# Projections of a two-layer hybrid trunk: products and transpositions one step later, norm weights in the rotation tables, roots applied by ScalarE

## The chip, the core and the metric

The kernel is one program on one core of a Trainium2 chip. The metric is the device time of one execution in microseconds (us). The engines are TensorE (PE; its weight loads are listed apart as PEld), VectorE (DVE), ScalarE (ACT), GpSimd (POOL) and SyncE (SP), which here mainly issues transfers (DMA). Each engine works through its own instructions in a fixed order.

## The reference

Two layers run over 1152 tokens (128 context, 1024 latent) of width 1024. Each modulates and normalises its input, projects it to four groups of heads, and joins them by one output projection. What the change touches is the modulation `silu(c) @ w_ada[l] + b_ada[l]`, the projection, and the head norm and rotation of grouped-query attention (GQA), beside the two norms of multi-head latent attention (MLA):

```python
shift, scale, gate = jnp.split(mod, 3, axis=-1)
h = rms_norm(x, p['norm_pre']) * (1 + scale) + shift
u = h @ p['w_in']
...
qa = rms_norm(gq.reshape(B, N, GQA_HEADS, HEAD_DIM), p['gqa_q_norm'])
ka = rms_norm(gk.reshape(B, N, GQA_KV_HEADS, HEAD_DIM), p['gqa_k_norm'])
...
qa_use = apply_axial_rope(qa, cos_h, sin_h)
...
cq = rms_norm(mcq, p['mla_q_norm'])
ckv = rms_norm(mckv, p['mla_kv_norm'])
```

The normalised context keys of GQA, unrotated, are an output as well (`o_gqa_k`).

## The kernel before

Tokens are worked in 9 tiles of 128. float32 products are made of three passes over high and low parts: `hh`, `hl` are the two parts of the modulated input, `whi`, `wlo` those of the weights (DVE casts `whi`, L235; POOL subtracts for `wlo`, L239; each from a loaded `wst`). A layer projects group after group: GLA values, SSD gates, MLA gates, the convolution's input (`proj_T`), GQA, MLA, then the query and key groups (QK); after these come attention and the two streams, and the output projection. `proj_tok` does 24 matmuls per token tile into one of four PSUM buffers taken in turn (two of `psA`, two of `psB`), hands the buffer to `consume`, and then draws one or two steps of `steps_`. So tile 4 of a projection needs the buffer that the consumer of tile 0 has read to its end.

`steps_` is the modulation for later: while layer 0 projects, `ada_steps` makes layer 0's gate and all of layer 1's modulation, in eight parts. A part takes eight loads `ast` of 256 KB (L163), each multiplied by the condition and summed to `acc` on DVE (L173), with ACT (L167, L170) and POOL (L171) beside it; then PE sums over the partitions into `psC`, which has one buffer (L180 for the gate, L186 else). Attention's `po` uses `psC` too.

The consumer of GQA, per tile: ACT copies the values to `vg` (L557) and squares the rest to `sq` (L559); DVE reduces to `ss` (L561); POOL makes the reciprocal roots (`rstd`, L106 and L107); DVE multiplies them onto the PSUM tile to `z` (L564), which is the last reading of that buffer; POOL multiplies `z` by the norm weights `g6` (L566); with a loaded tile `ropes` DVE (L574) and POOL (L577, twice) make the two parts of the rotation, DVE adds them to `r` (L581); PE transposes `r` to `gT` (L584), and ACT copies that to `qT` and `kT`.

The code gives no order between engines' instructions: a scheduler that models the engines' times fixes each engine's order when the program is built, so that a small edit can move rows far from it. Pools with `bufs=n` give out n buffers in turn; a new tile waits for the last reader of the old.

## Time and profile before

| | before |
|---|---|
| median of 3 runs | 1848.38 us (1847.5, 1848.38, 1854.49) |
| profiled execution, its own time | 1848.65 us |
| its span | 1846.8 us |
| PE busy | 1720.3 us (93%) |
| DVE busy | 1191.8 us (65%) |
| ACT busy | 867.2 us (47%) |
| POOL busy | 740.6 us (40%) |

Busy is the time in which an engine had an instruction under way; all four run side by side, so the shares are of the same span. Times in the trace count from the start of the span. The granted clock of PE stands as a share of its full 2.4 GHz, so 0.50 is its lower level, 1.2 GHz. In a row of the trace `out<-in` names the tiles by the program's names, and a releaser behind an arrow is what ended an engine's idle time.

### The profile page before, as it was taken

What the parts mean: (1) busy time and instruction counts of PE and PEld (TensorE: products, weight loads), DVE (VectorE), ACT (ScalarE), POOL (GpSimd) and SP (SyncE); (2) the same over time, 40 slices, a digit from 0 to 9 for tenths busy, and PEclk for the clock granted to TensorE, in tenths of its full rate; (3) what the DMA queues carried; (4) which work ended last, traced back from release to release, by engine and by line L of the source; (5) the groups of instructions that cost most, each with busy time, mean ns of one, the idle gap of its engine ahead of it and who ended that gap; (6) DMA issues with size and microseconds to landing.
All of it is one profiled execution on the core that took longest, in us unless ns stands there. A gap on an engine that the chain in (4) does not pass through costs nothing.

```text
span 1846.8 us, 25193 instructions
## 1 busy us (share of the span) xinstructions
PE 1720.3 (93%) x8200; PEld 1321.0 (72%) x8200; DVE 1191.8 (65%) x2302; ACT 867.2 (47%) x1914; POOL 740.6 (40%) x911
## 2 busy tenths in 40 slices
PE   6999989999999998999999999999999999999998
PEld 2787977887665666656777999889666666665676
DVE  7627888566877887782455357543686878677233
ACT  5634422433654665583443152232465477557322
POOL 4633238852444444330334323771344454333011
PEclk9999998999999999999999999999998999899999
DMA  8434453333332331142434332131332232114243
GB/s 290 134 97 139 140 158 90 106 111 99 109 99 73 87 97 49 38 149 60 143 118 129 99 101 86 56 101 43 111 117 84 68 98 86 46 38 149 80 143 114
DMA packets 179684, 190.99 MB, mean 103 GB/s; under 512 B 29406, under 2 KB 140720, under 8 KB 179552
## 3 DMA queue, kind: packets, MB, share of 16 engines
q1 hardware_dynamic: 174208, 179.11, 31.9%
q10 hardware_dynamic: 5344, 10.26, 1.8%
q8 instruction: 65, 1.06, 0.2%
q14 instruction: 67, 0.55, 0.1%
HBM read 141.00 MB, written 48.30 MB: 103 GB/s over the span
## 4 chain that ended last, share of the span: by engine, by line
PE 36%; DVE 11%; DMA 7%; POOL 4%; ACT 3%; issue 3%; SPq 0%; POOLq 0%; DVEq 0%; ACTq 0%
PE psP L245 11%; PE op L245 8%; PE st L1057 3%; PE po L1073 3%; DVE mx L711 2%; DMA R<-d_rec 2%; PE mx L710 1%; DVE Pl L1065 1%; DMA d_rec<-rc 1%; PE po L1069 1%; DMA wst<-in_w_in_dram 1%; PE po L1067 1%; PE po L1068 1%; POOL ss L107 1%; POOL sq L577 1%
## 5 line engine op out<-in xcount | busy, mean ns | idle before, releaser
L711 DVE TENSOR_REDUCE mx<-mx 128x1 f32<-128x512 f32 (+2 forms) x400 | 224.5, 582 | 93.6 <-PE mx L710 92.0
L245 PE MATMUL psP<-whi,hh 128*128 128x512 f32 (+2 forms) x576 | 204.9, 366 | 5.6 <-DVE whi L235 4.3
L245 PE MATMUL psP<-wlo,hh 128*128 128x512 f32 (+2 forms) x576 | 204.8, 363 | 3.4 <-POOL wlo L239 2.8
L245 PE MATMUL psP<-whi,hl 128*128 128x512 f32 (+2 forms) x576 | 188.4, 360 | 0.0
L239 POOL TENSOR_TENSOR wlo<-wst,whi 128x512 fp32r<-128x512 f32 (+3 forms) x106 | 128.9, 1224 | 141.5 <-DVE whi L235 82.4
L245 PE MATMUL psP<-hh,whi 128*128 128x384 f32 x480 | 163.0, 339 | 4.7 <-DVE whi L235 3.7
L1057 PE MATMUL st<-QA,KA 128*128 128x512 f32 (+1 forms) x336 | 165.2, 492 | 0.6 <-DVE Pl L1065 0.4
L245 PE MATMUL psP<-hl,whi 128*128 128x384 f32 x480 | 160.2, 335 | 0.0
L245 PE MATMUL psP<-hh,wlo 128*128 128x384 f32 x480 | 155.0, 337 | 0.1
L1065 DVE TENSOR_TENSOR Pl<-st,Ph 128x512 fp32r<-128x512 f32 x160 | 109.7, 686 | 67.2 <-ACT st L1063 66.0
L1062 ACT ACTIVATE Ph<-st 128x512 fp32r<-128x512 f32 x160 | 95.5, 597 | 111.2 <-PE st L1057 104.4
L1072 ACT ACTIVATE P<-st 128x512 f32<-128x512 f32 (+1 forms) x176 | 99.7, 567 | 74.4 <-PE st L1057 65.3
L1057 PE MATMUL st<-QB,KB 66*128 66x512 f32 (+3 forms) x336 | 133.2, 401 | 0.0
L245 PEld LDWEIGHTS psP<-wlo,hh 128*128 128x128 f32 x576 | 111.5, 195 | 21.3 <-POOL wlo L239 6.8
L245 PEld LDWEIGHTS psP<-whi,hh 128*128 128x128 f32 x576 | 111.6, 195 | 20.0 <-DVE whi L235 6.1
L245 PEld LDWEIGHTS psP<-whi,hl 128*128 128x128 f32 x576 | 109.5, 194 | 12.0
L1057 PEld LDWEIGHTS st<-QA,KA 128*128 128x128 f32 x336 | 65.8, 196 | 50.2 <-issue 39.8
L245 PEld LDWEIGHTS psP<-hh,whi 128*128 128x128 f32 x480 | 90.1, 188 | 11.9 <-DVE whi L235 5.6
L1057 PE MATMUL st<-QB,KA 96*128 96x512 f32 (+1 forms) x168 | 93.6, 557 | 2.2 <-ACT P L1072 1.8
L1063 ACT ACTIVATE st<-st 128x512 f32<-128x512 f32 x160 | 94.9, 593 | 0.0
L235 DVE CAST whi<-wst 128x512 fp32r<-128x512 f32 (+3 forms) x114 | 74.0, 662 | 31.8 <-DMA wst<-in_w_in_dram 19.2
L1073 PE MATMUL po<-P,vm 128*65 128x512 f32 (+1 forms) x176 | 88.9, 587 | 4.6 <-ACT P L1072 2.3
(361 smaller groups left out, 4315.6 us busy)
## 6 DMA issues: line engine op xcount, KB each, us to landing
ast<-in_w_ada_dram SPq DMA_DIRECT2D x96, 256.0 KB
wst<-in_w_in_dram SPq DMA_DIRECT2D x64, 256.0 KB
wost<-in_w_out_dram SPq DMA_DIRECT2D x16, 512.0 KB
d_xs<-d_xb SPq DMA_DIRECT2D x32, 192.0 KB
ot<-d_oT SPq DMA_DIRECT2D x18, 320.0 KB
d_tok<-vv SPq DMA_DIRECT2D x18, 256.0 KB
d_gt<-gg SPq DMA_DIRECT2D x24, 192.0 KB
g_qk<-d_qk SPq DMA_DIRECT2D x36, 128.0 KB
```

Source lines behind the costliest of these rows:

```text
L107: pool.tensor_tensor(out=rs, in0=rs, in1=mhalf[:, 0:c], op=ALU.pow)
L235: dve.tensor_copy(hi[:, 0:n], st[:, 0:n])
L239: eng.tensor_tensor(out=lo[:, 0:n], in0=st[:, 0:n], in1=hi[:, 0:n], op=ALU.subtract)
L245: pe.matmul(p, lhsT=lt, rhs=rh, start=(first and i == 0), stop=(last and i == n - 1))
L577: pool.tensor_tensor(out=ws_[:, :, x, :].rearrange("p (h y) f -> p h y f", y=2), in0=zs[:, :, 1 - x, :].rearrange("p (h y) f -> p h y f", ...
L711: dve.tensor_reduce(out=mx[:, t, i:i + 1], in_=p[:, 0:n], axis=AX.X, op=ALU.max)
L1057: anchors["pe"] = pe.matmul(sp_[:, 0:nq], lhsT=kx[:, ks], rhs=qx[:, qs], start=(i == 0), stop=(i == len(spasses) - 1))
L1062: act.activation(out=Ph[:, 0:nq], in_=sp_[:, 0:nq], func=AF.Exp, scale=scale)
L1063: anchors["act"] = act.activation(out=sp_[:, 0:nq], in_=sp_[:, 0:nq], func=AF.Exp, scale=scale)
L1065: anchors["dve"] = dve.tensor_tensor(out=Pl[:, 0:nq], in0=sp_[:, 0:nq], in1=Ph[:, 0:nq], op=ALU.subtract)
L1072: anchors["act"] = act.activation(out=P[:, 0:nq], in_=sp_[:, 0:nq], func=AF.Exp, scale=scale)
L1073: pe.matmul(po[0:65, 0:nq], lhsT=v[:, kt, vi, :], rhs=P[:, 0:nq], start=(j == 0), stop=last, skip_group_check=True)
```

## The change

Four edits. (1) `ast` has three buffers instead of two, and `ada_steps` yields once more between a part's last load and its product. (2) `consume` may return a function `rest`; `proj_tok` calls it after the next tile's matmuls. For GQA and MLA it holds the transpositions and the copies out of them. (3) The rotation table of all nine tiles is loaded at once, twice (`rg[0]` for queries, `rg[1]` for keys), and multiplied by the norm weights: the cosine halves in one product of 128x9x64 each (DVE for `rg[0]`, POOL for `rg[1]`), the sine halves in four products of 128x9x16 each on POOL. The product of every tile's `z` by `g6` goes, except that tile 0 makes one of 128x128 for `o_gqa_k`; per tile the rotation is two DVE and four POOL instructions where it was one and two. (4) The reciprocal roots are applied by ACT, one instruction of 128x64 for each of six heads, instead of one of 128x384 on DVE.

```diff
             o = part * D + half * 512
             acc = wpool.tile([128, 2, 512], F32, name="acc", tag="acc", bufs=1)
-                st = wpool.tile([128, 512], F32, name="ast", tag="ast", bufs=2)
+                st = wpool.tile([128, 512], F32, name="ast", tag="ast", bufs=3)
...
                 yield
+            yield
             p = psC("ada")
...
+        rest = None
...
             mm3(p[:, 0:n], pairs)
-            consume(t, p)
+
+            last, rest = rest, consume(t, p)
+            if last is not None:
+                last()
             for _ in range(2 - t % 2):
                 next(steps_[0], None)
+        if rest is not None:
+            rest()
...
+            rg = [wk.tile([128, T, 2, 64], F32, name="rg", tag=x) for x in ("c1h", "c1l")]
+            for i in range(2):
+                sp.dma_start(out=rg[i], in_=a["rope"][:, 0:128].rearrange("(t p) (y d) -> p t y d", p=128, d=64))
+            for i in range(2):
+                gi = g6[:, i * 256:i * 256 + 64]
+                gx = gi.rearrange("p (y x f) -> p y x f", x=2, f=16)
+                (pool if i else dve).tensor_tensor(out=rg[i][:, :, 0, :], in0=rg[i][:, :, 0, :], in1=gi.unsqueeze(1).to_broadcast([128, T, 64]),
+                                                   op=ALU.mult)
+                for x in range(2):
+                    for y in range(2):
+                        o = 32 * y + 16 * x
+                        z = rg[i][:, :, 1, o:o + 16]
+                        pool.tensor_tensor(out=z, in0=z, in1=gx[:, y, 1 - x, :].unsqueeze(1).to_broadcast([128, T, 16]), op=ALU.mult)
             def cons_gqa(t, p):
                 kt = 0 if t == 0 else t + 2
-                ropes = wk.tile([128, 192], F32, name="ropes", tag="ropes", bufs=2)
-                sp.dma_start(out=ropes, in_=a["rope"][t * 128:(t + 1) * 128, :])
                 act.copy(vg[:, kt, :, 0:64], p[:, 384:512].rearrange("p (h d) -> p h d", d=64))
                 sq = wk.tile([128, 384], F32, name="sq", tag="sq", bufs=2)
                 act.activation(out=sq, in_=p[:, 0:384], func=AF.Square)
@@ -561,29 +581,35 @@
                 dve.tensor_reduce(out=ss, in_=sq.rearrange("p (h d) -> p h d", d=64), axis=AX.X, op=ALU.add)
                 rstd(ss, ss, 64, 6)
                 z = wk.tile([128, 384], F32, name="z", tag="z", bufs=2)
-                dve.tensor_tensor(out=z.rearrange("p (h d) -> p h d", d=64), in0=p[:, 0:384].rearrange("p (h d) -> p h d", d=64),
-                                  in1=ss.unsqueeze(2).to_broadcast([128, 6, 64]), op=ALU.mult)
-                pool.tensor_tensor(out=z, in0=z, in1=g6, op=ALU.mult)
+                for h in range(6):
+                    c = slice(h * 64, h * 64 + 64)
+                    act.activation(out=z[:, c], in_=p[:, c], func=AF.Identity, scale=ss[:, h:h + 1])
+                r = wk.tile([128, 384], F32, name="r", tag="r", bufs=2)
                 if t == 0:
-                    act.dma_start(out=a["o_gqa_k"][l], in_=z[:, 256:384])
+                    pool.tensor_tensor(out=r[:, 256:384], in0=z[:, 256:384], in1=g6[:, 256:384], op=ALU.mult)
+                    act.dma_start(out=a["o_gqa_k"][l], in_=r[:, 256:384])
                     act.dma_start(out=a["o_gqa_v"][l].rearrange("t (h d) -> t h d", d=64), in_=vg[:, 0, :, 0:64])
-                r = wk.tile([128, 384], F32, name="r", tag="r", bufs=2)
-                zs = z.rearrange("p (h x f) -> p h x f", x=2, f=16)
-                ws_ = sq.rearrange("p (h x f) -> p h x f", x=2, f=16)
-                rs_ = ropes[:, 64:128].rearrange("p (y x f) -> p y x f", x=2, f=16)
-                dve.tensor_tensor(out=r.rearrange("p (h d) -> p h d", d=64), in0=z.rearrange("p (h d) -> p h d", d=64),
-                                  in1=ropes[:, 0:64].unsqueeze(1).to_broadcast([128, 6, 64]), op=ALU.mult)
-                for x in range(2):
-                    pool.tensor_tensor(
-                        out=ws_[:, :, x, :].rearrange("p (h y) f -> p h y f", y=2),
-                        in0=zs[:, :, 1 - x, :].rearrange("p (h y) f -> p h y f", y=2),
-                        in1=rs_[:, :, x, :].unsqueeze(1).to_broadcast([128, 6, 2, 16]), op=ALU.mult)
+                    r = wk.tile([128, 384], F32, name="r", tag="r", bufs=2)
+                for i, (o, n) in enumerate(((0, 4), (256, 2))):
+                    c = slice(o, o + n * 64)
+                    dve.tensor_tensor(out=r[:, c].rearrange("p (h d) -> p h d", d=64), in0=z[:, c].rearrange("p (h d) -> p h d", d=64),
+                                      in1=rg[i][:, t, 0, :].unsqueeze(1).to_broadcast([128, n, 64]), op=ALU.mult)
+                    zs = z[:, c].rearrange("p (h y x f) -> p h y x f", x=2, y=2, f=16)
+                    ws_ = sq[:, c].rearrange("p (h y x f) -> p h y x f", x=2, y=2, f=16)
+                    rs_ = rg[i][:, t, 1, :].rearrange("p (y x f) -> p y x f", x=2, f=16)
+                    for x in range(2):
+                        pool.tensor_tensor(out=ws_[:, :, :, x, :], in0=zs[:, :, :, 1 - x, :],
+                                           in1=rs_[:, :, x, :].unsqueeze(1).to_broadcast([128, n, 2, 16]), op=ALU.mult)
                 dve.tensor_tensor(out=r, in0=r, in1=sq, op=ALU.add)
-                tp = psD("gT")
-                for i in range(3):
-                    pe.transpose(tp[:, i * 128:(i + 1) * 128], r[:, i * 128:(i + 1) * 128], ident)
-                act.copy(qT[:, :, t * 128:(t + 1) * 128], tp[:, 0:256].rearrange("p (a b) -> p a b", b=128))
-                act.copy(kT[:, kt * 128:(kt + 1) * 128], tp[:, 256:384])
+                def rest():
+                    tp = psD("gT")
+                    for i in range(3):
+                        pe.transpose(tp[:, i * 128:(i + 1) * 128], r[:, i * 128:(i + 1) * 128], ident)
+                    act.copy(qT[:, :, t * 128:(t + 1) * 128], tp[:, 0:256].rearrange("p (a b) -> p a b", b=128))
+                    act.copy(kT[:, kt * 128:(kt + 1) * 128], tp[:, 256:384])
+                return rest
...
-                tp = psD("mT")
...
+                def rest():
+                    tp = psD("mT")
+                    pe.transpose(tp[:, 0:128], z[:, 0:128], ident)
+                    pe.transpose(tp[0:64, 128:256], z[:, 128:192], ident)
+                    pe.transpose(tp[:, 256:384], z[:, 192:320], ident)
...
+                return rest
```

Lines after the change stand 1 to 30 higher. Three places show how rows moved.

At the start of layer 0's GQA, the rows of SP before (transfers in the order of issue; `d_bc` is the convolution's output, `wst` of 128x352 are MLA's weights):

```order
L163 DMA ast<-in_w_ada_dram 128x512
L535 DMA d_bc_430<-yc 128x128
L536 DMA d_bc_430<-yc 128x1024
L163 DMA ast<-in_w_ada_dram 128x512
L233 DMA wst<-in_w_in_dram 128x352
L556 DMA ropes<-in_rope_dram 128x192 x2
L163 DMA ast<-in_w_ada_dram 128x512
L233 DMA wst<-in_w_in_dram 128x352
```

and now:

```order
L234 DMA wst<-in_w_in_dram 128x352
L542 DMA d_bc_430<-yc 128x128
L543 DMA d_bc_430<-yc 128x1024
L234 DMA wst<-in_w_in_dram 128x352
L563 DMA rg<-in_rope_dram 128x9x128 x2
L635 DMA ropes<-in_rope_dram 128x192 x2
L116 DMA bc<-in_b_col_dram 128x16
L163 DMA ast<-in_w_ada_dram 128x512 x8
```

The two tables stand after both MLA weights, and the `ast` loads that were mixed with the weights stand behind the tables. At the same place POOL had, from GQA's last weights on:

```order
L239 TENSOR_TENSOR wlo<-wst,whi 128x512 x8
L106 TENSOR_SCALAR ss_2491<-ss_2491 128x6
L107 TENSOR_TENSOR ss_2491<-ss_2491,mhalf 128x6
L106 TENSOR_SCALAR ss_2549<-ss_2549 128x6
L107 TENSOR_TENSOR ss_2549<-ss_2549,mhalf 128x6
L566 TENSOR_TENSOR z<-z,g_1037 128x384
L577 TENSOR_TENSOR sq<-z,ropes 128x12x16 x2
L566 TENSOR_TENSOR z<-z,g_1037 128x384
```

and has now:

```order
L240 TENSOR_TENSOR wlo<-wst,whi 128x512 x8
L573 TENSOR_TENSOR rg<-rg,g_1037 128x9x16 x4
L567 TENSOR_TENSOR rg<-rg,g_1037 128x9x64
L573 TENSOR_TENSOR rg<-rg,g_1037 128x9x16 x4
L106 TENSOR_SCALAR ss_2491<-ss_2491 128x6
L106 TENSOR_SCALAR ss_2550<-ss_2550 128x6
L107 TENSOR_TENSOR ss_2491<-ss_2491,mhalf 128x6
L107 TENSOR_TENSOR ss_2550<-ss_2550,mhalf 128x6
L601 TENSOR_TENSOR sq<-z,rg 128x8x16 x2
L589 TENSOR_TENSOR r<-z,g_1037 128x128
L601 TENSOR_TENSOR sq<-z,rg 128x4x16 x2
```

All nine products of the tables stand ahead of the first reciprocal root (the small step L106 and the root L107), and the tiles' products with `g` have gone.

In layer 1's GQA POOL had:

```order
L239 TENSOR_TENSOR wlo<-wst,whi 128x512 x8
L106 TENSOR_SCALAR ss_11451<-ss_11451 128x6
L107 TENSOR_TENSOR ss_11451<-ss_11451,mhalf 128x6
L106 TENSOR_SCALAR ss_11501<-ss_11501 128x6
L107 TENSOR_TENSOR ss_11501<-ss_11501,mhalf 128x6
L566 TENSOR_TENSOR z<-z,g_10181 128x384 x2
L577 TENSOR_TENSOR sq<-z,ropes 128x12x16 x4
```

and has now:

```order
L240 TENSOR_TENSOR wlo<-wst,whi 128x512 x8
L106 TENSOR_SCALAR ss_11524<-ss_11524 128x6
L107 TENSOR_TENSOR ss_11524<-ss_11524,mhalf 128x6
L573 TENSOR_TENSOR rg<-rg,g_10242 128x9x16 x4
L106 TENSOR_SCALAR ss_11575<-ss_11575 128x6
L601 TENSOR_TENSOR sq<-z,rg 128x8x16
L589 TENSOR_TENSOR r<-z,g_10242 128x128
L601 TENSOR_TENSOR sq<-z,rg 128x8x16
L567 TENSOR_TENSOR rg<-rg,g_10242 128x9x64
L573 TENSOR_TENSOR rg<-rg,g_10242 128x9x16 x4
L107 TENSOR_TENSOR ss_11575<-ss_11575,mhalf 128x6
L601 TENSOR_TENSOR sq<-z,rg 128x4x16 x2
```

Four table products stand between the first tile's root and the second tile's small step; the other five stand ahead of the second tile's root.

At the start of layer 0's attention, PE had from the last modulation product on (`st` are score matmuls, `mx` the same for the maxima, `po` the products with the values):

```order
L245 MATMUL psP<-hh,wlo 128x384
L180 MATMUL ada<-acc,pick 2x512
L1057 MATMUL st<-QA_3697,KA_3695 128x128
L1057 MATMUL st<-QB_3698,KB_3696 128x128
L710 MATMUL mx<-KA_3695,QA_3697 128x512 x2
L710 MATMUL mx<-KA_3695,QA_3697 128x256
L1057 MATMUL st<-QA_3697,KA_3695 128x512
L1057 MATMUL st<-QB_3698,KB_3696 128x512
L1057 MATMUL st<-QA_3697,KA_3695 128x512
L1057 MATMUL st<-QB_3698,KB_3696 128x512
L1073 MATMUL po<-P,vg 65x128
```

and has now, further down its list:

```order
L1087 MATMUL st<-QB_3724,KB_3722 128x512
L757 MATMUL mT<-identr,m 2x128
L740 MATMUL mx<-KA_3721,QA_4372 128x512
L181 MATMUL ada<-acc,pick 2x512
L1087 MATMUL st<-QA_3723,KA_3721 128x512
L1087 MATMUL st<-QB_3724,KB_3722 128x512
L740 MATMUL mx<-KA_3721,QA_4372 128x512
L1103 MATMUL po<-P,vg 65x128
L1103 MATMUL po<-P,vg 65x512
L1097 MATMUL po<-Ph,vh 65x512
```

The last modulation product stood ahead of the first 512-wide `st`; now the scores of several blocks are ahead of it (those rows are left out here), and the first `po` follows it.

## Rows read from the trace of the kernel before

**Rows 1.** Windows: busy us of PE, PEld, DVE, ACT, POOL; PE clock, DMA, GB/s

```profile
140.00:285.00 145.00, 135.56 (x709) 120.45 (x708) 115.37 (x159) 54.22 (x93) 50.03 (x53) 0.95 0.48 143
285.00:335.00 50.00, 43.20 (x209) 36.42 (x208) 39.23 (x54) 12.44 (x34) 45.67 (x46) 0.93 0.38 107
1155.00:1205.00 50.00, 48.06 (x236) 40.34 (x235) 29.42 (x42) 11.42 (x35) 41.48 (x50) 1.00 0.22 63
```

**Rows 2.** Waits of PE in 130-145, 260-285, 285-335, 1180-1250: us, times, longest

```profile
PE ada L180 <- DVE acc L173: 3.2, 1, 3.2
...
PE ada L186 <- DVE acc L173: 3.9, 1, 3.9
...
PE gT L584 <- DVE r L581: 4.4, 2, 2.6
PE psP L245 <- DVE whi L235: 1.7, 3, 0.7
...
PE gT L584 <- DVE r L581: 1.1, 1, 1.1
PE psP L245 <- DVE z L564: 0.9, 2, 0.7
```

**Rows 3.** Windows, columns as in rows 1, around three of PE's waits

```profile
136.60:143.40 6.80, 6.23 (x20) 4.52 (x20) 1.60 (x5) 1.99 (x5) 1.27 (x1) 0.50 0.35 110
277.44:283.40 5.96, 5.96 (x15) 4.70 (x16) 5.09 (x6) 1.33 (x2) 5.80 (x7) 0.50 0.34 94
314.10:317.50 3.40, 3.40 (x13) 3.04 (x12) 2.10 (x4) 0.84 (x2) 3.40 (x5) 0.50 0.20 53
```

**Rows 4.** Waits of DVE in 110-138: us, times, longest

```profile
DVE acc L173 <- DMA ast<-in_w_ada_dram: 8.6, 6, 3.9
```

**Rows 5.** Timeline, 262-278: start, us, engine, line, op [idle before <-releaser]

```profile
262.92 1.68 POOL L239 TENSOR_TENSOR wlo<-wst,whi 128x512 fp32r<-128x512 f32 x1 [1.02 <-issue]
...
265.17 0.33 SPq L163 DMA_DIRECT2D ast<-in_w_ada_dram  x1
...
268.54 2.84 DVE L173 SCALAR_TENSOR_TENSOR acc<-ast,cc,acc 128x512 f32<-128x512 f32 x4 [1.88 <-DMA ast<-in_w_ada_dram]
...
275.00 0.21 POOL L106 TENSOR_SCALAR ss<-ss 128x6 f32<-128x6 f32 x1 [10.40 <-DVE ss L561]
275.29 1.34 POOL L107 TENSOR_TENSOR ss<-ss,mhalf 128x6 f32<-128x6 f32 x1
...
277.44 0.77 PE L245 MATMUL psP<-whi,hh 128*128 128x512 f32 x1
```

**Rows 6.** Timeline of PE at the start of layer 0's attention

```profile
440.90 1.07 PE L1073 MATMUL po<-P,vg 128*65 128x512 f32 x2 [1.48 <-ACT Ou L1084]
```

**Rows 7.** ACT by form: busy us, mean ns | idle before; and two copies in the timeline

```profile
L218 ACT ACTIVATE h<-hT,sc,ac 128x128 f32<-128x128 f32 x36 | 15.4, 455 | 18.9 <-DVE h L221 18.6
L167 ACT ACTIVATE acc<-ast,cc 128x512 f32<-128x512 f32 x4 | 2.7, 714 | 7.8 <-PE ada L186 7.8
...
271.32 0.44 ACT L557 COPY vg<-psP 128x128 f32<-128x128 f32 x2
```

**Rows 8.** The page's part 3: queue, packets, MB, share of 16 engines

```profile
q1 hardware_dynamic: 174208, 179.11, 31.9%
```

**Rows 9.** POOL by form, 1150-1250, columns as in rows 7

```profile
L577 POOL TENSOR_TENSOR sq<-z,ropes 128x192 f32<-128x192 f32 x18 | 14.2, 810 | 0.2
L566 POOL TENSOR_TENSOR z<-z,g 128x384 f32<-128x384 f32 x9 | 9.0, 1014 | 0.7 <-DVE z L564 0.7
L629 POOL TENSOR_TENSOR r<-z,ropes 128x16 f32<-128x16 f32 x18 | 3.6, 220 | 0.0
```

**Rows 10.** Timeline of SP, POOL and PE in layer 1's GQA

```profile
1158.43 8.57 SPq L556 DMA_DIRECT2D ropes<-in_rope_dram  x4
...
1158.18 0.21 POOL L106 TENSOR_SCALAR ss<-ss 128x6 f32<-128x6 f32 x1 [4.50 <-DVE ss L561]
...
1169.28 0.49 PE L584 MATMUL gT<-ident,r 128*128 128x128 f32 x3
```

More of the change, by code (lines that the diff above doesn't have):

```diff
@@ L630, in cons_mla @@
                 pool.tensor_tensor(out=kr, in0=kr, in1=r[:, 0:32], op=ALU.add)
-                tp = psD("mT")
-                pe.transpose(tp[:, 0:128], z[:, 0:128], ident)
-                pe.transpose(tp[0:64, 128:256], z[:, 128:192], ident)
-                pe.transpose(tp[:, 256:384], z[:, 192:320], ident)
-                s = slice(t * 128, (t + 1) * 128)
-                act.copy(c1h[:, s], tp[:, 0:128])
-                dve.tensor_tensor(out=c1l[:, s], in0=tp[:, 0:128], in1=c1h[:, s], op=ALU.subtract)
-                act.copy(c2s[0:64, s], tp[0:64, 128:256])
-                dve.tensor_tensor(out=c2s[64:128, s], in0=tp[0:64, 128:256], in1=c2s[0:64, s], op=ALU.subtract)
-                s = slice(kt * 128, (kt + 1) * 128)
-                act.copy(ckh[:, s], tp[:, 256:384])
-                dve.tensor_tensor(out=ckl[:, s], in0=tp[:, 256:384], in1=ckh[:, s], op=ALU.subtract)
+                def rest():
[3 more added lines that the diff above has]
+                    pe.transpose(tp[:, 256:384], z[:, 192:320], ident)
+                    s = slice(t * 128, (t + 1) * 128)
+                    act.copy(c1h[:, s], tp[:, 0:128])
+                    dve.tensor_tensor(out=c1l[:, s], in0=tp[:, 0:128], in1=c1h[:, s], op=ALU.subtract)
+                    act.copy(c2s[0:64, s], tp[0:64, 128:256])
+                    dve.tensor_tensor(out=c2s[64:128, s], in0=tp[0:64, 128:256], in1=c2s[0:64, s], op=ALU.subtract)
+                    s = slice(kt * 128, (kt + 1) * 128)
+                    act.copy(ckh[:, s], tp[:, 256:384])
+                    dve.tensor_tensor(out=ckl[:, s], in0=tp[:, 256:384], in1=ckh[:, s], op=ALU.subtract)
+                return rest
             proj_tok(l, hh, hl, wp, G_MLA, 352, cons_mla)
```

## The prediction

> **What bounds the kernel now.** I read the busy table, then the stages by windows, then the waits of TensorE (PE) stage by stage, then single engines where a wait ended. PE is busy 93% of the span, so only its gaps and its time at the lower clock can be won. The windows say where: in 140 to 285 us PE is busy 135.6 of 145, but in 285 to 335, the GQA and MLA projections of layer 0, 43.2 of 50, while POOL is busy 45.7 of 50; in layer 1 the same stage has PE at 48.1 of 50 and POOL at 41.5 [rows 1]. The waits name the links [rows 2]: a modulation product waits 3.2 us for DVE's sum at 137; another 3.9 us at 270 to 274; at the end of GQA the `gT` transpositions wait 4.4 us for the rotated `r`, and weights 1.7 us for DVE's casts; layer 1 has 1.1 and 0.9 us. After such waits PE's granted clock is 0.50, its lower level, for some microseconds [rows 3]. Half of PE's busy time in such a stretch is the most that full clock would give back: 3.1 us of 6.23 after the first wait (I take 2.5, since part of that busy time is the product's own pass at the wait's end), 3.0 of 5.96 after 277.44, 1.7 at 314 and, in a like stretch, 1.7 at 331.
>
> All the waits and clock losses that the change can touch are thus 3.2 + 2.5, 3.9 + 3.0, 6.1 + 3.4 and 2.0: 24 us, or 1.3%, is the ceiling.
>
> **The change part by part.** I sum against the profiled run's 1848.65 us (span 1846.8), which stands 0.3 above the median of 1848.38.
>
> *Third `ast` buffer.* Ahead of the product at 137 DVE waited 8.6 us, 6 times, for `ast` loads [rows 4]: with two buffers a load is issued only when a sum frees one. A load takes from its issue at 265.17 to DVE's use at 268.54, 3.4 us [rows 5]. With one more in flight the chain of eight loses about one such load, which covers the 3.2 us. The product stands at almost the same PE row before and after, so the wait should vanish with its half clock: -5.7 us (0 if POOL's sums were the limit, -6.3 with all the clock).
>
> *Products one step later.* The extra yield moves work back: eight parts of eight loads and two yields need 80 steps where layer 0's projections offer 72, so the last part is drained at the end of QK. PE's rows show the last product only after the first `st` of attention, and every `po` behind it, because `psC` has one buffer. There PE already waited, 1.5 us at 440.90 for ACT [rows 6]. I give this +1 us (0 if ACT and DVE set the pace anyway; +4 if one last load of 3.4 us lies bare).
>
> *`z` on ACT.* DVE loses one multiplication per tile, ACT gets six of 128x64. The trace has no such row. The nearest, ACT with a scale per partition: 128x128 0.455 us, 128x512 0.714 [rows 7]; slope 0.67 ns per element, so 0.41 for 64. Six would be 2.5 us end to end. Two ACT copies of 128x128 at 271.32 took 0.44 us together though one takes 0.27: they overlap by 0.10, so I take 1.9; at the copies' spacing of 0.17 six would be 1.1, the lower bound. ACT was idle over half of these stages, so only the delay counts: a PSUM buffer comes free, and the rotation starts, about 1.3 us later than by DVE's 0.56.
>
> The Trainium skill ("ScalarE: Activation LUTs", Rules for kernel authors) speaks against this edit: it gives multiplications to VectorE and budgets about 0.3 us per ACTIVATE plus 0.83 ns per element, by which six would take 2.1 us (an estimate from that page). Its price is inside the bounds from the rows; by it each of the two GQA starts below comes 0.2 us later, and the sum ends at -7.8 instead of -8.2. No run here yet shows 64 columns.
>
> *Folded tables.* Two loads of 590 KB in 512-byte pieces (1152 each) replace nine of 96 KB. Queue q1's 174208 packets of 1028 bytes on average took 31.9% of 16 engines' span, 54 ns each [rows 8]; 1152 over 16 engines are 3.9 us at that price and 1.9 if time goes with bytes. The 3.4 us of an `ast` load, less the 0.9 us of its packets at 54 ns and 1028 bytes, leave 2.5 us of delay. The first table then lands 4.4 us after its issue, the second 1.9 later (at the upper bounds 6.4 and 3.9). On POOL stand eight multiplications of 9x16 and one of 9x64: 16 elements took 0.220 us, 192 took 0.810, 384 in one piece 1.014 [rows 9]. Between these, 144 take 0.65 and, on the last slope of 2.16 ns, 576 take 1.43: 6.6 us of setup per layer (bounds 5.5 if all had that slope, 7.3 at twice the fixed part). Per tile the product with `g6` goes (1.01), but four rotations of 128 and 64 elements (0.60 and 0.38 by the same rows) cost 1.96 where two of 192 cost 1.62. POOL wins 0.67 us per tile, 6 us in nine: no more than the setup costs. What matters is when it is paid.
>
> *Layer 0, GQA start.* POOL stood idle 10.4 us before its first `rstd` at 275.00 [rows 5], so the setup is partly free. SP issues the tables after the second MLA weight, which needs the last GQA `wlo`. That began at 262.92 [rows 5]; its cast no longer stands behind sums, so I put `wlo`'s end at 262.2 and the tables' issue at 262.6. First table 267.0; four products to 269.6; 1.43 to 271.0; four more to 273.6; two `rstd` steps and a root of 1.34 to 275.3; `z` to 277.2. Tile 4 needs `z` of tile 0 for its PSUM buffer. Before it started at 277.44 [rows 5], behind the 3.9 us wait and 16 products at half clock. So the wait for the product goes and a wait for `z` of the same length takes its place: -0.2 (-2 to +4). That is the step that most people would book as a gain.
>
> *Layer 0, tail.* From here POOL, busy 91% of this stage before, has 0.67 us less per tile, the four sums of L171 stand later, and the transpositions are issued after the next tile's matmuls. POOL is through at least 6 us earlier, which is all that the waits for `r` and the weights came to, and PE's own 24 matmuls per tile set the pace. Of 6.1 + 3.4 I take -8 (-4 to -9.5).
>
> *Layer 1, GQA start.* No modulation, and before no PE gap. Now POOL's rows put the first four table products ahead of tile 1's `rstd`, and the other five ahead of its root. The tables take the place of `ropes` at 1158.43 [rows 10]: landing 1162.8, four products 1165.4, two rotations, the `o_gqa_k` product and a small step (1.9) 1167.3, 9x64 1168.7, four products 1171.3, root 1172.6, two rotations 1173.4, DVE's sum 1174.0. `gT` of tile 0 stood at 1169.28 [rows 10] and now waits to 1174.1; tile 5 waits for `z` of tile 1, 1174.5. That is +5.0 us (+2.5 to +7), +1.7 for the clock that sinks after it, and, since PE is then later than POOL's end, -2.0 for the tail's two waits [rows 2]: +4.7.
>
> Sum: -5.7 + 1.0 - 0.2 - 8.0 + 4.7 = -8.2, so **1840.4 us**. The order of attention and streams in layer 0 is rescheduled too; I have no row that prices it and keep 5 us to each side for it.
>
> **Rivals.** A difference under 0.5% (9.2 us) can't be told from no change.
>
> *The setup is hidden* (0.15). If the tables land early and the small products cost less than 0.5 us, layer 1 keeps its gapless start, layer 0's tile 4 starts some 5 us earlier, and both tails go whole: -5.7 + 1 - 5 - 9.4 - 2 = -21, 1827.5. For it: POOL's 10.4 idle us. Against it: in layer 1 POOL was idle only 4.5 us before its first `rstd` [rows 10], and the tables can't start before `d_bc` is written.
>
> *The stalls only change their name* (0.25). At the upper bounds of the table loads, layer 0's start costs +3, its tail gives -6, layer 1 +7: -5.7 + 1 + 3 - 6 + 7 = -0.7, 1848. For it: all setup stands in front of `rstd`, the head of the chain.
>
> *Slower* (0.14). The mechanism is the table landing late in both layers, as SP holds it behind weights that wait for POOL. POOL is in order, so `rstd`, `z`, the PSUM buffers and PE wait with it, microsecond for microsecond in each layer. From -8.2 it takes (8.2 + 9.2) / 2 = 8.7 us in each to be slower by 0.5%: a landing at 276 and 1171.5. The bounds above give only about 3.4; I keep the chance for that and the unpriced order of attention. At 11 us late it is 1862.
>
> **How the numbers follow.** The forecast has 0.46, with its own range 1835 to 1846. Of it two fifths (0.19) lie below 1839.2; with the hidden setup (0.15) and a little of the second rival (0.02) faster gets 0.36. Slower gets 0.14 + 0.02, no change 0.48. The range 1828 to 1854 leaves out half of the first rival (0.08) and most of the last (0.12).
>
> **What would show it.** No wait before the product at 137, the granted clock there 1.0; a PE gap of 4 to 8 us before tile 4 of GQA in layer 0, ended by ACT's `z`; no `gT` gaps after it; in layer 1 a new gap of about 5 us at `gT` or tile 5; six ACT instructions of 0.3 to 0.41 us per tile; table products of 0.65 us on POOL. It is wrong if tile 4 starts before 273 or after 282 (in these coordinates, less the shift from 137), if layer 1 shows no gap, or if attention of layer 0 moves by more than 5 us.

## The result and the profile after

The changed kernel takes 1860.07 us (median of 16 runs, 1853.36 to 1867.45) where the kernel before takes 1847.14 in as many; the ratio is 1.0072 with a 95% interval of 1.0055 to 1.0089. It is slower, outside the range I had given. Its profiled execution, with a span of 1853.8 us against 1846.8, is one of its quicker ones, 7 us above the profiled one of before where the medians differ by 13. The four stages below add up to +10.6; the rest of the kernel, mostly what follows in layer 1, is 3.6 us shorter.

Windows over the stages, first of the changed kernel: layer 0 from its first projection to GQA, from GQA to the end of QK, attention with streams and output projection, and layer 1 from GQA to the end of QK. Columns as in [rows 1].

```profile
46.20:232.90 186.70, 178.72 (x998) 159.98 (x997) 120.73 (x205) 88.44 (x171) 79.10 (x83) 0.99 0.44 133
232.90:421.90 189.00, 175.64 (x926) 154.89 (x925) 118.58 (x202) 68.16 (x223) 112.19 (x156) 0.95 0.38 110
421.90:972.90 551.00, 505.94 (x2209) 348.48 (x2208) 383.31 (x790) 310.01 (x656) 211.01 (x250) 0.96 0.30 93
1147.60:1317.90 170.30, 163.82 (x867) 147.48 (x866) 82.19 (x156) 54.73 (x202) 86.76 (x145) 0.97 0.24 71
```

The same four stages of the kernel before:

```profile
46.60:243.50 196.90, 184.46 (x997) 163.35 (x996) 124.89 (x204) 88.58 (x171) 77.76 (x83) 0.96 0.42 124
243.50:435.20 191.70, 179.88 (x928) 157.54 (x928) 130.38 (x205) 58.83 (x172) 115.99 (x140) 0.96 0.37 111
435.20:967.70 532.50, 497.63 (x2208) 344.90 (x2206) 370.01 (x783) 306.91 (x653) 201.28 (x245) 0.98 0.31 95
1141.70:1307.00 165.30, 160.80 (x867) 144.57 (x866) 87.63 (x155) 43.38 (x148) 88.06 (x126) 1.00 0.24 71
```

The projections of layer 0 give 10.2 and 2.7 us back. Layer 1's cost 5.0. But the third stage, whose code the change does not touch, takes 18.5 us more: for the same matmuls (2209 and 2208) PE is busy 8.3 us longer, at a lower clock, and idle 45.1 instead of 34.9. That alone turns a gain into a loss.

PE's waits after, in 125 to 135, 260 to 300, 300 to 345 and 1147 to 1250, answering to [rows 2]:

```profile
PE ada L181 <- DVE acc L173: 0.9, 1, 0.9
...
PE psP L246 <- ACT z L586: 8.4, 1, 8.4
...
PE mT L660 <- DVE z L641: 3.3, 1, 3.3
...
PE gT L608 <- DVE r L603: 4.0, 1, 4.0
```

The product's wait at 137 is nearly gone, and so are the `gT` waits of GQA's tail in layer 0. New are a wait for ACT's `z` in the place of that for the second product, one of MLA's transposition, and one of layer 1's first `gT`.

The timeline at layer 0's GQA start, which answers to [rows 5]; the second fence shows layer 1, which answers to [rows 10]:

```profile
251.31 1.79 SPq L563 DMA_DIRECT2D rg<-in_rope_dram  x2
...
256.62 2.34 POOL L573 TENSOR_TENSOR rg<-rg,g 128x144 f32<-128x144 f32 x4 [5.71 <-DMA rg<-in_rope_dram]
259.10 1.40 POOL L567 TENSOR_TENSOR rg<-rg,g 128x576 f32<-128x576 f32 x1
260.46 3.16 POOL L573 TENSOR_TENSOR rg<-rg,g 128x144 f32<-128x144 f32 x4
...
264.60 2.64 POOL L107 TENSOR_TENSOR ss<-ss,mhalf 128x6 f32<-128x6 f32 x2
...
267.37 0.79 PE L246 MATMUL psP<-whi,hh 128*128 128x512 f32 x1 [8.41 <-ACT z L586]
```

```profile
1164.33 1.93 SPq L563 DMA_DIRECT2D rg<-in_rope_dram  x2
...
1169.88 2.56 POOL L573 TENSOR_TENSOR rg<-rg,g 128x144 f32<-128x144 f32 x4 [3.55 <-DMA rg<-in_rope_dram]
...
1175.46 1.87 POOL L573 TENSOR_TENSOR rg<-rg,g 128x144 f32<-128x144 f32 x4
...
1177.30 1.32 POOL L107 TENSOR_TENSOR ss<-ss,mhalf 128x6 f32<-128x6 f32 x1
1178.59 0.59 POOL L601 TENSOR_TENSOR sq<-z,rg 128x64 f32<-128x64 f32 x2
...
1179.21 0.56 DVE L603 TENSOR_TENSOR r<-r,sq 128x384 f32<-128x384 f32 x1 [3.11 <-POOL sq L601]
...
1179.83 0.90 PE L608 MATMUL gT<-ident,r 128*128 128x128 f32 x3 [4.05 <-DVE r L603]
```

The tables reach POOL 5.3 and 5.6 us after their issue, and the nine products follow. In layer 0 the roots, ACT's `z` and PE come next; in layer 1 the second tile's root, the first tile's last rotations, DVE's sum to `r` and PE. The chain is the predicted one in both layers. Around the wait that ends at 1179.83 PE's clock is 0.50 for 6.8 us, as it is around MLA's (323.25):

```profile
322.10:328.90 6.80, 5.65 (x20) 5.62 (x21) 4.78 (x11) 1.68 (x8) 4.67 (x10) 0.50 0.60 165
1178.80:1185.60 6.80, 5.77 (x15) 4.67 (x16) 3.92 (x8) 4.61 (x20) 5.98 (x12) 0.50 0.00 0
```

At MLA's first `mT`, DVE's timeline shows six sums, one waiting for its load, ahead of the `z` that the transposition needs:

```profile
318.80 4.07 DVE L173 SCALAR_TENSOR_TENSOR acc<-ast,cc,acc 128x512 f32<-128x512 f32 x6 [2.55 <-DMA ast<-in_w_ada_dram]
322.78 0.41 DVE L641 SCALAR_TENSOR_TENSOR z<-psP,ss,gq 128x192 f32<-128x192 f32 x1
...
323.25 0.48 PE L660 MATMUL mT<-ident,z 128*128 128x128 f32 x1 [3.27 <-DVE z L641]
```

In layer 0's attention (421.9 to 838.6) these waits of PE lead the list:

```profile
PE mx L740 <- DVE mx L741: 7.1, 11, 1.4
PE mT L757 <- DVE m L754: 6.8, 5, 2.3
PE kT L887 <- DVE g_kq L879: 6.6, 5, 1.7
PE po L1099 <- DVE Pl L1095: 4.1, 4, 1.7
```

Before (435.2 to 832.2) it was:

```profile
PE mx L710 <- DVE mx L711: 7.4, 9, 2.9
PE po L1069 <- DVE Pl L1065: 4.7, 6, 3.0
PE mT L727 <- DVE m L724: 4.2, 3, 3.1
...
PE kT L857 <- DVE g_kq L849: 1.3, 2, 0.8
```

No single wait carries the loss. There are more of them, and longer: over the third stage the trace has 18 gaps of PE over 1 us where it had 9, and 44.4 us at clock 0.50 where it had 23.9. Half of the 20.5 us more, 10.3, is the most that the lower clock can add to PE's busy time; it is 8.3 us busier.

### The profile page after: what moved, and what is told of

Same layout as the page of the kernel before. It is cut to its first block, busy times and chain, and to the rows that moved or that the text cites. A ratio compares the mean times of both kernels' runs of the same rounds, so it can differ in the third digit from the quotient of the medians.

```text
span 1853.8 us, 25318 instructions
## 1 busy us (share of the span) xinstructions
PE 1715.5 (93%) x8200; PEld 1317.7 (71%) x8200; DVE 1185.7 (64%) x2304; ACT 891.3 (48%) x2022; POOL 742.0 (40%) x949
## 4 chain that ended last, share of the span: by engine, by line
PE 57%; DVE 15%; DMA 11%; POOL 6%; issue 5%; ACT 4%; SPq 1%; POOLq 0%; DVEq 0%; ACTq 0%
PE psP L246 22%; PE op L246 8%; PE st L1087 5%; PE po L1103 4%; PE mx L740 3%; DVE mx L741 2%; DMA R<-d_rec 2%; DMA wst<-in_w_in_dram 1%; PE att L895 1%; PE po L1099 1%; DVE Pl L1095 1%; DMA d_rec<-rc 1%; PE go L916 1%; DMA ast<-in_w_ada_dram 1%; PE po L1097 1%
```

## The experiments

Theory A: the extra yield leaves a modulation part over, and the scheduler then writes layer 0's attention and streams in another, slower order. Theory B: the table setup costs the time, and the long attention of one profile is chance. Each ratio is to executions of the kernel before that ran beside that run (their medians are 1843.65 to 1847.14 us), on three chips for e1 to e4, e5 to e8 and e9 to e12; so it is the ratios that are compared, not the medians of two rows. The last two columns are windows of each run's profile: layer 0 from the end of QK to layer 1's first projection, and layer 1 from GQA to the end of QK.

| run | median us | ratio to before beside it | 95% | attention and output, layer 0 | GQA to QK, layer 1 |
|---|---|---|---|---|---|
| before | 1847.14 | | | 532.5 | 165.3 |
| changed | 1860.07 | 1.0072 | 1.0055 to 1.0089 | 551.0 | 170.3 |
| e1 yield, buffer alone | 1858.98 | 1.0060 | 1.0042 to 1.0078 | 548.2 | 165.3 |
| e2 without the yield | 1843.24 | 0.9973 | 0.9955 to 0.9992 | 532.1 | 168.4 |
| e3 80 draws | 1843.45 | 0.9964 | 0.9945 to 0.9983 | 530.1 | 170.5 |
| e4 no folding, 80 draws | 1849.53 | 0.9999 | 0.9979 to 1.0020 | 530.0 | 165.3 |
| e5 one draw more | 1843.49 | 0.9985 | 0.9962 to 1.0008 | 532.7 | 172.8 |
| e6 product in psD | 1840.45 | 0.9988 | 0.9970 to 1.0005 | 534.5 | 168.1 |
| e7 folding in layer 0 only | 1842.37 | 0.9991 | 0.9973 to 1.0009 | 530.9 | 166.7 |
| e8 half the tables on DVE | 1838.93 | 0.9962 | 0.9943 to 0.9981 | 533.7 | 166.3 |
| e9 no deferral, 80 draws | 1847.38 | 1.0002 | 0.9984 to 1.0020 | 530.6 | 172.8 |
| e10 z on DVE, 80 draws | 1848.95 | 1.0018 | 1.0000 to 1.0036 | 531.1 | 173.7 |
| e11 e7 and e8 together | 1840.36 | 0.9966 | 0.9946 to 0.9987 | 530.4 | 169.2 |
| e12 e11, psD, 72 draws | 1853.51 | 1.0033 | 1.0018 to 1.0048 | 551.2 | 165.3 |

**e1**: the kernel before with two edits.

```diff
-                st = wpool.tile([128, 512], F32, name="ast", tag="ast", bufs=2)
+                st = wpool.tile([128, 512], F32, name="ast", tag="ast", bufs=3)
...
                 yield
+            yield
             p = psC("ada")
```

> The kernel before with only the third ast buffer and the extra yield; GQA and MLA as before. Its PE rows in layer 0's attention are those of the changed kernel, all 1449 alike. Theory A (the extra yield leaves one modulation part to be drained at the end of QK, and the scheduler then writes layer 0's attention in another, slower order): the projections of layer 0 give back 4 to 8 us, attention and streams of layer 0 (end of QK to the first output projection) take about 417 us instead of 397, and the kernel is 10 to 15 us slower than before. Theory B (the table setup of GQA costs the time, and the longer attention of the one profile is chance): 3 to 6 us faster than before, attention of layer 0 within 4 us of 397.

0.6% slower, with 548.2 us: two edits that do not touch attention's code bring nearly the whole loss (1.0060 of 1.0072). Theory A holds.

**e2**: the changed kernel without the yield.

```diff
                 yield
-            yield
             p = psC("ada")
```

> The changed kernel without the extra yield (the third ast buffer stays). Its PE rows in layer 0's attention are those of the kernel before, all 1449 alike. Theory A: attention of layer 0 takes about 397 us again, layer 1's GQA keeps its loss of about 7 us, and the kernel comes to 0 to 8 us faster than before. Theory B: still 8 us or more slower than before.

The third stage is back at 532.1 and the kernel faster than before, with the table setup still in it; B falls. Layer 1 keeps 3.1 us of its loss in this profile, not 7.

**e3**: the yield kept, but all 80 steps drawn in time.

```diff
-            for _ in range(2 - t % 2):
+            for _ in range(2 if off in (G_SM, G_MLA) else 2 - t % 2):
```

> The changed kernel with two steps drawn for every token tile in the SSD-gate and MLA projections, so that all 80 steps, the extra yields among them, are drawn before QK ends. PE rows of layer 0's attention as before the change, all 1449 alike. Theory A: as the run without the yield, 0 to 8 us faster than before, attention of layer 0 about 397 us: the yield itself costs nothing, only the part left over and the order that follows from it. Theory B: 8 us or more slower than before.

As e2: the yield as such costs nothing.

**e4**: e3 with the GQA consumer of before (its transpositions deferred).

```diff
-            rg = [wk.tile([128, T, 2, 64], F32, name="rg", tag=x) for x in ("c1h", "c1l")]
...
             def cons_gqa(t, p):
+                ropes = wk.tile([128, 192], F32, name="ropes", tag="ropes", bufs=2)
...
-                for h in range(6):
-                    c = slice(h * 64, h * 64 + 64)
-                    act.activation(out=z[:, c], in_=p[:, c], func=AF.Identity, scale=ss[:, h:h + 1])
...
+                pool.tensor_tensor(out=z, in0=z, in1=g6, op=ALU.mult)
```

> The third buffer, the extra yield and the deferred transpositions with 80 draws, but GQA's rotation, norm weights and roots as before. Theory A with the table setup as the second cost: layer 1's GQA has no new gap, so 5 to 9 us less than the run of the changed kernel with 80 draws, and 6 to 14 us faster than before. If the folding were a gain, this run would be slower than that one.

A miss. Layer 1's gap goes as expected, but the run is no faster than before: GQA to QK of layer 0 takes 196.1 us here, 190.7 in e3. So in these two profiles the folded consumer earns in layer 0 (5.4 us) what it costs in layer 1 (5.2). By the ratios e4 is some 0.35% slower than e3, which by the expectation's last sentence makes the folded consumer, `z` on ACT included, a gain. The `gT` waits of layer 0 are still there (3.1 us, before 4.4), so deferring the transpositions does not remove them by itself. Its attention rows are not exactly those of before (some 1400 of 1449).

**e5**: one step more is drawn.

```diff
-            for _ in range(2 - t % 2):
+            for _ in range((2 if t % 2 and (off == G_SM and t // 2 < 1 or off == G_MLA and t // 2 < 0) else 2 - t % 2)):
```

> The changed kernel with one step more drawn, in the SSD-gate projection (tile 1). Seven of the eight steps of the last modulation part instead of all eight are left for the end of QK, so nearly the same work is drained there, but PE's rows in layer 0's attention are those of the kernel before again, all 1449 alike. If the drained work itself (loads, sums on DVE, the held psC) costs the time, attention of layer 0 stays above 410 us and the kernel within 3 us of the changed one. If it is the order that the scheduler falls into, attention of layer 0 takes about 396 us and the kernel 1840 to 1846.

The sharpest one. Seven steps left over instead of eight, PE's order of attention that of before, and 532.7 us instead of 551.0. The drained work is not the cost; the order is.

**e6**: another place for the last product.

```diff
-            p = psC("ada")
+            p = psD("ada") if (part, half) == (2, 1) and l else psC("ada")
```

> The changed kernel with all its 80 steps over 72 draws, but the last part's product in psD, which has three buffers, so that no po of attention waits for it. The order becomes a third one: the first po at PE place 1977 instead of 2003, 710 of 1449 rows in layer 0's attention as in the changed kernel, 581 as before. If the held psC is the cost, attention of layer 0 falls to 396 to 402 us; if the loss lies in the order behind the start, it stays between 402 and 417.

534.5 us, a third order, and a fast one, though all eight steps are drained late. DVE is as busy in it as in the changed kernel's (382.47 and 383.31 us in the rows here and above), so that DVE has more to do there isn't the cause either. Taken alone it would fit a held `psC`: attention up to the first matmul of the output projection takes 398.4 us, within what was expected for that. e12 and a look at the changed kernel below bear on it.

The third stage of e1, e3, e5, e6 and e12, by windows, in this order:

```profile
422.80:971.00 548.20, 506.35 (x2211) 347.89 (x2209) 386.26 (x787) 310.32 (x656) 210.08 (x249) 0.96 0.30 93
```

```profile
427.90:958.00 530.10, 496.96 (x2209) 345.32 (x2207) 365.83 (x784) 306.90 (x653) 203.28 (x246) 0.98 0.31 96
```

```profile
428.50:961.20 532.70, 499.86 (x2207) 346.26 (x2206) 367.46 (x784) 307.05 (x652) 204.47 (x246) 0.97 0.31 95
```

```profile
423.50:958.00 534.50, 495.76 (x2208) 343.00 (x2208) 382.47 (x787) 308.69 (x656) 209.27 (x250) 0.98 0.31 95
```

```profile
425.10:976.30 551.20, 507.05 (x2210) 350.92 (x2210) 370.28 (x784) 307.24 (x653) 204.17 (x246) 0.96 0.30 92
```

The reader is to compare length less PE's busy time, and the clock: 42 and 44 us idle at 0.96 in the slow ones (e1, e12), 33 to 39 at 0.97 or 0.98 in the others. Over all profiles of this stage, the changed kernel, e1 and e12 have 41.0 to 44.4 us at clock 0.50 and 13 to 18 gaps of PE over 1 us; the other ten runs and the kernel before have 17.1 to 30.7 us and 9 or 10 gaps.

**e7**: e3 with `if l == 0` around the folded consumer, and the one of before, deferred, in layer 1.

```diff
+            if l == 0:
...
+                def cons_gqa(t, p):
...
+            else:
+                def cons_gqa(t, p):
+                    kt = 0 if t == 0 else t + 2
+                    ropes = wk.tile([128, 192], F32, name="ropes", tag="ropes", bufs=2)
```

> The run with 80 draws, with the folded tables and ACT's roots in layer 0 alone; layer 1's GQA works as before the change (with deferred transpositions). If the table setup ahead of layer 1's roots costs what the traces show (GQA 59.2 us against 51.9, MLA 37.9 against 41.5), this is 2 to 5 us faster than that run: 1838 to 1842. If layer 1's gap were paid back elsewhere, it is the same within 2 us.

The stage behaves (166.7), but the total is not the expected 2 to 5 us faster: by the ratios e7 is, if anything, 0.3% slower than e3, at the edge of the error.

**e8**: e3 with the query table's small products on DVE.

```diff
-                        pool.tensor_tensor(out=z, in0=z, in1=gx[:, y, 1 - x, :].unsqueeze(1).to_broadcast([128, T, 16]), op=ALU.mult)
+                        (pool if i else dve).tensor_tensor(out=z, in0=z, in1=gx[:, y, 1 - x, :].unsqueeze(1).to_broadcast([128, T, 16]), op=ALU.mult)
```

> The run with 80 draws, with the four small products of the query table on DVE instead of POOL, so that five products are left on POOL and both layers' roots come about 2.4 us earlier. If the setup on POOL is what tile 4 of GQA waits for, its PE gap in layer 0 falls from about 8 to 5 or 6 us, layer 1's gap from 4 to about 2, and the kernel is 2 to 7 us faster than the run with 80 draws. If the landing of the tables sets it, the gaps fall by less than 1 us.

Layer 1 from GQA to QK falls from 170.5 to 166.3, and its `gT` wait from 4.0 us to two of 0.8 together, which confirms POOL's setup as the cause there; the other seven profiles with the folding in layer 1 lie at 168.1 to 173.7. In layer 0 PE waits as long as in e3 (7.6 and 7.4 us), but the trace names DVE's sum for the product there: in that order the sums, not the roots, end last. With 0.9962 it is faster than both kernels, but not the expected 2 to 7 us faster than e3: the two can't be told apart.

**e9**: e3 with `consume`'s rest called at once.

```diff
-            last, rest = rest, consume(t, p)
+            last = consume(t, p)
```

> The run with 80 draws, but GQA's and MLA's transpositions and copies issued at once, as before the change. PE rows of layer 0's attention as before, all 1449 alike. If the deferral is what empties GQA's tail, gT waits of 1 to 3 us come back at the end of GQA and this is 3 to 8 us slower than the run with 80 draws. If POOL's lighter tiles emptied it, the two are the same within 2 us; if the deferral only moved the wait to mT in MLA (3.7 us there), it is 2 to 5 us faster.

0.4% slower than e3 by the ratios, yet no `gT` wait comes back, and MLA's `mT` still waits 3.9 us (3.7 in e3). So the folded consumer, with POOL's lighter tiles, emptied the tail, and not the deferral; e4 has the deferral without the folding, and its `gT` waits stay. Where the 0.4% lies I can't show: the profiles differ by 2.3 us in layer 1 from GQA to QK and by less in the other stages listed.

**e10**: e3 with `z` by one DVE instruction again.

```diff
-                for h in range(6):
-                    c = slice(h * 64, h * 64 + 64)
-                    act.activation(out=z[:, c], in_=p[:, c], func=AF.Identity, scale=ss[:, h:h + 1])
+                dve.tensor_tensor(out=z.rearrange("p (h d) -> p h d", d=64), in0=p[:, 0:384].rearrange("p (h d) -> p h d", d=64),
+                                  in1=ss.unsqueeze(2).to_broadcast([128, 6, 64]), op=ALU.mult)
```

> The run with 80 draws, but the roots applied by DVE in one instruction of 128x384 as before the change. Six ACT instructions took 1.34 us in the changed kernel, DVE's one 0.56 before. If the delay of z on ACT matters, both GQA starts come 0.8 us earlier and this is 1 to 4 us faster. If DVE's load matters more (5 us of work per layer comes back to it), it is 1 to 4 us slower. Within 2 us I can't tell them apart.

0.5% slower than e3, more than was expected either way: ACT's six instructions are a gain, though tile by tile they take longer than DVE's one:

```profile
1163.50 0.56 DVE L584 TENSOR_TENSOR z<-psP,ss 128x384 f32<-128x384 f32 x1 [2.58 <-POOL ss L107]
```

As with e9, e3 was not run again beside it, so the comparison goes over the kernel before.

**e11**: e7 with e8's edit.

```diff
-                            pool.tensor_tensor(out=z, in0=z, in1=gx[:, y, 1 - x, :].unsqueeze(1).to_broadcast([128, T, 16]), op=ALU.mult)
+                            (pool if i else dve).tensor_tensor(out=z, in0=z, in1=gx[:, y, 1 - x, :].unsqueeze(1).to_broadcast([128, T, 16]), op=ALU.mult)
```

> 80 draws, tables folded in layer 0 alone, the query table's sine products on DVE. The two single steps gave 0.9991 and 0.9962 of before where 80 draws alone gave 0.9964; if they add, 1835 to 1840 and layer 1's GQA at 51.9 us. If layer 1's stage is all that is won, about 3 us less than the run with half the setup on DVE.

0.9966, within the error of e3 and e8: the single gains don't add visibly. Its layer 1, where the folding is off, takes 169.2 us, and e12's, with the same code there, 165.3:

```profile
1137.40:1306.60 169.20, 164.74 (x865) 147.50 (x864) 87.86 (x155) 43.35 (x148) 88.04 (x126) 0.97 0.24 70
1236.90:1247.10 10.20, 9.22 (x27) 6.82 (x26) 3.54 (x9) 1.80 (x7) 6.43 (x10) 0.50 0.45 131
```

```profile
1151.20:1316.50 165.30, 160.81 (x867) 144.68 (x866) 87.33 (x155) 43.39 (x148) 88.02 (x126) 1.00 0.24 71
```

PE's waits are the same in both (`gT` 1.1 us, `mT` 1.0, `psP` 0.9 twice) and so is its idle time, 4.5 us; but in e11 the clock stood at 0.50 for 10.2 us. A stage of a single profile is thus good to some 4 us, and smaller differences between stages here are not to be trusted by themselves; the 15 to 19 us of the third stage are clear of that.

**e12**: e11 with 72 draws and e6's edit.

```diff
-            p = psC("ada")
+            p = psD("ada") if (part, half) == (2, 1) and l else psC("ada")
...
-            for _ in range(2 if off in (G_SM, G_MLA) else 2 - t % 2):
+            for _ in range(2 - t % 2):
```

> As the run before it, but with 72 draws, so that all of the last modulation part is drained at the end of QK, and its product in psD. The order of layer 0's attention is one more: 793 of 1449 rows as before the change, 739 as in the changed kernel, first po at PE place 1977. If a held psC is what made the changed kernel's attention slow, attention takes 395 to 401 us here too and the kernel 1835 to 1842; if orders near the changed kernel's are slow by themselves, it takes 402 us or more.

551.2 us with `psC` free and DVE no busier than before the change. This order is slow as well. A held `psC` is thus not needed for a slow order, and likeness to either order (793 and 739 rows) doesn't tell a fast one from a slow one: e6, with 581 and 710, is fast. By the expectation's own measure, up to the output projection's first matmul, e12 is only just slow (402.2 us); but in its order more of attention stands behind that matmul (54 `st` and 50 `po`, instead of 45 and 41), so the whole stage is the fairer measure.

That a held `psC` isn't what slows the changed kernel's own order, e12 can't show. Its trace bears on it: here is its third stage up to the first `po`, and the same 19.0 us of the kernel before.

```profile
421.90:440.93 19.03, 13.58 (x35) 6.17 (x35) 12.81 (x24) 11.61 (x23) 10.08 (x13) 0.75 0.16 50
```

```profile
435.20:454.20 19.00, 14.51 (x53) 8.10 (x52) 14.31 (x29) 10.47 (x23) 9.95 (x15) 0.91 0.52 150
```

PE is idle 5.5 us here, and 4.5 before; 9.2 of the 10.2 us of more idle time come after `po` has its buffer. PE is 18 matmuls behind by then, some 4 us (an estimate, from 505.94 us for 2209), so the larger part of the 18.5 us is lost later.

## Why the prediction was wrong

*Third buffer, -5.7.* Right. PE's wait fell from 3.2 to 0.9 us, the clock stayed at 1.0 through 260, and the SSD-gate stage, from its first matmul to the next group's, went from 37.8 to 32.6 us: -5.2. Some 5 us more came in other stages before GQA, which I had not counted; part of them is scatter, for e1 and e6, with the same code up to GQA, take 190.5 and 188.4 us there instead of 186.7.

*Products one step later, +1 (0 to +4), and 5 us to each side for the order.* This is the step that failed. I priced the last product's place in the queue (it comes at 437.69, and the first `po` of attention at 440.93; PE waits 1.1 us for the product before it and not at all for the last), but took the rescheduling of 1449 PE rows behind it as noise of 5 us. It was the largest term: +18.5 us in this pair, +15.7 in e1, and 17 to 20 us between the changed kernel and e2 or e3, by medians or by ratios. I had seen that the rows were rescheduled and had no row to price them by, so I set a small bound instead of leaving them unpriced. The last of the prediction's own signs of being wrong is the one that came: attention of layer 0 moved by 19.7 us, from 397.0 to 416.7.

```profile
427.63 1.67 PE L181 MATMUL ada<-acc,pick 128*2 128x512 f32 x2 [1.11 <-DVE acc L173]
...
437.69 1.86 PE L181 MATMUL ada<-acc,pick 128*2 128x512 f32 x2
...
440.93 0.63 PE L1103 MATMUL po<-P,vg 128*65 128x128 f32 x2
```

*`z` on ACT.* Too dear: by these two rows of the changed kernel (the groups of ACT between 255 and 330, then the timeline at layer 1's GQA), one takes 0.322 us where I had 0.41, and six start to end 1.34 (1.9 predicted, in bounds). They overlap by 0.12, hardly more than the copies' 0.10; most of the difference lies in the single instruction.

```profile
L586 ACT ACTIVATE z<-psP,ss 128x64 f32<-128x64 f32 x54 | 12.0, 322 | 21.0 <-POOL ss L107 21.0
```

```profile
1166.37 1.34 ACT L586 ACTIVATE z<-psP,ss 128x64 f32<-128x64 f32 x6 [1.46 <-POOL ss L107]
```

The budget in the Trainium skill ("ScalarE: Activation LUTs", Rules for kernel authors), about 0.3 us per ACTIVATE and 0.83 ns per element, gives 0.35 us for one of these (an estimate from that page), and the trace agrees with 0.322; but six times it, the 2.1 us of the prediction, is too much for six in a row. The same rules of the Trainium skill give multiplications to VectorE as the faster engine per element, and the trace agrees for the single tile (0.56 us in e10, 1.34 on ACT); the whole kernel is 0.5% slower with it there.

*Folded tables.* Right in kind. The tables came 5.3 to 5.6 us after their issue (4.4 predicted, 6.4 the bound); a product of 144 took 0.47 to 0.79 us in the means of four (0.65), one of 576 1.40 to 1.43 (1.43).

*Layer 0, GQA start, -0.2.* Right: PE waits 8.4 us for `z`, in place of the wait for the product.

*Layer 0, tail, -8.* Half right. The `gT` waits went, but a wait of 3.3 us and its low clock came at MLA's `mT`, where sums that wait for `ast` stand ahead of `z` on DVE; and QK carries the part left over. GQA to QK gave 2.7 us, not 8.2. And e1, which has only the buffer and the yield, is shorter there (186.4 us against 189.0). Its windows from GQA to the end of QK, of GQA and of MLA, then GQA and MLA of the changed kernel:

```profile
236.40:422.80 186.40, 175.39 (x926) 155.29 (x925) 124.44 (x203) 56.97 (x169) 113.32 (x137) 0.97 0.38 111
236.40:293.50 57.10, 54.70 (x259) 44.52 (x257) 43.00 (x54) 11.71 (x31) 39.72 (x37) 1.00 0.41 120
293.50:349.00 55.50, 48.07 (x285) 45.99 (x282) 36.07 (x74) 16.80 (x78) 38.31 (x69) 0.91 0.35 99
```

```profile
232.90:298.90 66.00, 56.79 (x264) 46.31 (x263) 42.09 (x61) 21.61 (x78) 47.62 (x61) 0.92 0.40 114
298.90:349.40 50.50, 46.34 (x281) 44.15 (x279) 29.34 (x68) 18.88 (x90) 31.73 (x70) 0.93 0.39 107
```

So with 72 draws GQA is 8.9 us longer with the folded tables, about the length of the wait for `z` (8.4), and MLA gives 5.0 back. By the ratios (1.0060 and 1.0072) edits 2 to 4 bring no difference to e1 that can be told.

*Layer 1, +4.7.* Right in its mechanism: a wait of 4.0 us (5.0 predicted), and 3.0 us more busy time at a lower clock (1.7 predicted). That the stage comes to +5.0 is in part luck: four other profiles with the same code there (e2, e3, e5, e6) lie at +2.8 to +7.5. Half the setup on DVE takes most of it away (e8).

The rival that ended slower had the wrong mechanism: the tables were not late enough; its 0.14 held a part for the unpriced order, which is what came. What remains open is why one order has more long waits than another; the traces show the waits and the clock behind them, not the scheduler's reasons.

## What to carry to other kernels

Where a scheduler places the instructions, compare its rows far beyond the edited lines, and treat a stage whose rows are reshuffled as unpriced: here 3.4% of a stage (551.0 us against 532.7) hung on one step left over. Count the steps against the draws when work is moved by a step; one draw more (e5), eight more (e3) or no extra yield (e2) gave the old, quick order of attention again and turned a ratio of 1.0072 into 0.9964 to 0.9985. A wait that is removed at a chain's head shows what the next wait is: price the second one before the gain is booked.

## What the runs showed of the hardware

Back-to-back ACT instructions of 128x64 with a scale per partition start about 0.20 us apart, (1.34 - 0.32) / 5, though each is on record with 0.32. In the changed kernel's third stage PE's waits cost nearly twice their length: 10.2 us more idle came with 20.5 us more at the lower clock and 8.3 us more busy time for the same matmuls. That is no fixed price: e6 is idle 3.9 us longer there than the kernel before, at the lower clock 17.1 us instead of 23.9, and only 2.0 us longer in all; and e11 and e12 have the same waits in layer 1, yet differ by 3.9 us of PE's busy time, because the clock fell in one and not in the other.
